# Starting the seven-product projections with one token block, and moving the Fourier values into them

## The chip, the cores and the metric

One core of a Trainium2 chip runs the whole program. The metric is the device time of one execution in microseconds (us), the median of several runs.

## The reference

One encoder layer, on a prompt of 256 tokens and a sample of 2048 tokens with the same weights, width 1024, all in float32. `trunk` is called once for each:

```python
xn = rmsnorm(x, norm_in);  mn = rmsnorm(mem, norm_mem)
pv, pg, fv, fg, q, ag, mg = split_cols(xn @ w_in)      # 1024, 1024, 512, 512, 512, 512, 3072 columns
ya = (pool_mixer(pv, w_pool_grp, pool_scale) * silu(pg)) @ w_pool_out
yb = (fourier_mixer(fv, w_four_grp) * silu(fg)) @ w_four_out
yc = (memory_xattn(q, mn, w_kv) * silu(ag)) @ w_attn_out
ga, gb, gc = split(sigmoid(mg + b_gate), 3)
y = rmsnorm(x + (ga * ya + gb * yb + gc * yc) @ w_o, norm_f)
```

The pooling mixer is a centred window mean less the token, times a matrix per group of 256 columns. The Fourier mixer is the real part of a two-dimensional transform over the tokens and the 128 columns of each of four groups, times a matrix per group. The attention goes to 256 memory tokens per request.

## The kernel before

Every product of two float32 matrices is made of three matmuls on high and low halves (`SPLITS`); making the halves is a cast on ACT and a subtraction on DVE (`split`, lines 98 and 99). The 2304 tokens are nine chunks of 256 and three blocks of 768 (`NB`). The engines' work stands in program order, and each engine works in its order; loads of weights and of intermediate tiles are issued on SP (`st`, line 120), and most stores and loads of intermediate values on POOL's queue.

The stages in order:

- **Opening and Fourier values.** The pooling matrices are multiplied into the pooling columns of `w_in` in 16 steps ("folds", lines 262 to 288, tiles `ptr`, `pvT`, `pfold`, `wfold`), eight at the start and eight at the end of the stage; the result goes to DRAM as `wp_d`. Chunk by chunk the tokens are normalized (`prep`, line 301), turned by eight transposes for each 128 tokens (`transpose8`, line 318) and split into `xc`. The first three chunks' operands go to DRAM as `xq_d`, in the seven combinations that the products later need; the other six chunks go there as plain turned tokens, `xr_d`. The Fourier columns of the chunk are 96 plain matmuls (`fv_mm`, lines 368 to 374), and `fv_post` folds the sample's tokens about their middle into `fe` and `fo`, in SBUF. Four tiles of memory tokens are turned in between.
- **Fourier transform.** Four groups of columns; in each a level of sums (`leaf_odd`, `leaf_even`, on POOL and DVE), short matmuls (`u_step`), the transform's matmuls (`dft_odd`, `dft_even`) and recombination (`comb_odd`, `comb_even`, lines 545 to 591), whose results SP stores to `fo_d`, `fe_d`, `fp_d`.
- **Memory values and keys**: `pv` (line 664) and `pk` (line 680), 96 matmuls each.
- **Products.** The projections go by pairs of weight tiles (class `Pair`, line 779): a 2x2 block product by seven products instead of eight (`PROD`), 12 matmuls of 128x384 each (line 830), accumulated in PSUM tiles x, y and z. There are 26 pairs in each of three blocks, 26 x 7 x 12 x 3 = 6552 matmuls. The x sum of a pair is emptied by ACT (`keep`, line 836) within two products. The activations (`act`, line 843) are Silu and Sigmoid. The Fourier gate multiplies the transform's result there (`gate_four`) and goes to `zb_d`. A small planner puts other work beside the products by its cost (`beside`, `side`, `debt`): the next block's operands (`x_prep`, from `xr_d`) and the pooling mixer (`pooling`) of the block before. `ALONE` and `ORDER` give the order of the seven products within a pair, alone or interleaved with the next pair.
- **Output.** Block by block: the Fourier branch (`pyb`), attention (`ps`), its branch (`pyc`), the pooling branch (`pya`, all line 1095) with gates, the output matrix (`pwo`, line 1290), the residual and the final norm. The mixer of block 2 runs here, in the pooling stage of blocks 0 and 1.

Of the kernel before, what the change touches and what calls it, by code (L numbers as in the profile page):

```python
# [11 lines left out]
F32 = mybir.dt.float32  # L12
# [5 lines left out]
P = 128  # L18
# [3 lines left out]
NB = 3  # L22
# [10 lines left out]
def tile_hybrid_encoder(  # L33
# [23 lines left out]
    def temp(name):  # L57
        return perm.tile([P, D], F32, tag="temp", name=name, bufs=7)
# [23 lines left out]
    vecT = perm.tile([P, 32], F32, tag="vecT", name="vecT")  # L82
# [86 lines left out]
    e_pv, e_fv, e_tok = [[], []], [], {}  # L169
    chunks = [0, 1, 8, 2, 7, 3, 6, 4, 5]  # L170
    MEM_AT = {2: 0, 3: 1, 5: 2, 6: 3}
    e_pv[0].append(st.add(w_in[0:P, PV0:PV0 + 512], 512))
    e_wp = [st.add(w_pool[0:512, :].rearrange("(a p) f -> p a f", p=P))]
    for d in range(1, 8):
        e_pv[0].append(st.add(w_in[d * P:(d + 1) * P, PV0:PV0 + 512], 512))
        if d >= 6:
            e_fv.append(st.add(ftile(w_in, FV0 + (d - 6) * P)))
    e_fv += [st.add(ftile(w_in, FV0 + g * P)) for g in (2, 3)]
    for ci in range(1, len(chunks)):
        for j in range(2):  # L180
# [15 lines left out]
    pairs += [((w_in, Q0 + h * P, "q", h), (w_in, AG0 + h * P, "ag", h)) for h in range(4)]
    for k in (1, 2, 0):
        pairs += [((w_in, MG0 + 1024 * k + c * P, "g", 8 * k + c), (w_in, MG0 + 1024 * k + (c + 4) * P, "g", 8 * k + c + 4))
                  for c in range(4)]
# [9 lines left out]
    n_pair = len(st.src)  # L209

# [32 lines left out]
    fh = rp.tile([P, 4, 4], F32, tag="fh", name="fh")
# [1213 lines left out]
```

## Time and profile before

| | us |
|---|---|
| time, median of three runs | 2136.88 (2136.13 to 2138.97) |
| the profiled execution | 2138.15 |
| its span | 2136.4 |
| TensorE busy | 2066.0 (97%) |
| VectorE (DVE) busy | 1404.8 (66%) |
| ScalarE (ACT) busy | 971.7 (45%) |
| GpSimd (POOL) busy | 421.0 (20%) |

The profile shows one execution; it stands 1.27 us above the median of the runs, and its span leaves out 1.75 us around the program. PE in the trace is TensorE's matmuls, SPq the part of SP that issues DMAs. A row of the timeline gives start, length, engine, line of the kernel, operation, output and inputs, the tile's shape and how often it is repeated; in brackets the idle time before it and what ended it. A group of instructions gives busy us, mean ns of one, and the idle time before them by what ended it. Stages lie at 0 to 191.5 us (opening and values), to 238.6 (transform), to 283.4 (values and keys of the memory), to 1436.7 (products) and to the end.

### The profile page before, as it was taken

What the parts mean: (1) busy time and instruction counts of PE and PEld (TensorE: products, weight loads), DVE (VectorE), ACT (ScalarE), POOL (GpSimd) and SP (SyncE); (2) the same over time, 40 slices, a digit from 0 to 9 for tenths busy, and PEclk for the clock granted to TensorE, in tenths of its full rate; (3) what the DMA queues carried; (4) which work ended last, traced back from release to release, by engine and by line L of the source; (5) the groups of instructions that cost most, each with busy time, mean ns of one, the idle gap of its engine ahead of it and who ended that gap; (6) DMA issues with size and microseconds to landing.
All of it is one profiled execution on the core that took longest, in us unless ns stands there. A gap on an engine that the chain in (4) does not pass through costs nothing. (4 is left out here: it accounts for less than half of the span.)

```text
span 2136.4 us, 31880 instructions
## 1 busy us (share of the span) xinstructions
PE 2066.0 (97%) x12087; PEld 2013.5 (94%) x12087; DVE 1404.8 (66%) x2243; ACT 971.7 (45%) x1785; POOL 421.0 (20%) x700
## 2 busy tenths in 40 slices
PE   7899989999999999999999999998999899999998
PEld 6898879999999999999999999998998899889997
DVE  5765647876555778888656888645675668566553
ACT  5653324655454556555544555546223622344131
POOL 1215213421001244221201212111111111111000
PEclk8999989999999999999999999999999999999999
DMA  8974997975338689676844867457968576876732
GB/s 296 325 231 156 301 235 212 284 207 160 128 121 291 190 243 282 199 220 202 296 143 145 237 199 218 158 200 241 303 209 300 188 261 215 288 237 219 226 118 90
DMA packets 358671, 468.65 MB, mean 219 GB/s; under 512 B 17045, under 2 KB 288437, under 8 KB 358261
## 3 DMA queue, kind: packets, MB, share of 16 engines
q0 software_dynamic: 111952, 261.27, 38.5%
q1 hardware_dynamic: 245792, 203.45, 30.9%
q8 instruction: 95, 1.56, 0.3%
q10 hardware_dynamic: 772, 1.88, 0.3%
q14 instruction: 60, 0.48, 0.1%
HBM read 310.83 MB, written 155.71 MB: 218 GB/s over the span
## 5 line engine op out<-in xcount | busy, mean ns | idle before, releaser
L830 PE MATMUL gx<-xo,wS 128*128 128x384 f32 x2808 | 508.3, 335 | 5.6 <-ACT s L836 4.4
L830 PEld LDWEIGHTS gx<-xo,wS 128*128 128x128 f32 x2808 | 491.0, 189 | 6.5 <-ACT s L836 5.0
L98 ACT CAST hl<-raw 128x1024 fp32r<-128x1024 f32 (+1 forms) x116 | 101.0, 874 | 305.7 <-PE pya L1095 94.3
L1095 PE MATMUL pya<-za,hl 128*128 128x384 f32 x1152 | 200.2, 334 | 0.0
L1095 PEld LDWEIGHTS pya<-za,hl 128*128 128x128 f32 x1152 | 199.7, 188 | 0.0
L830 PE MATMUL gz<-xo,wS 128*128 128x384 f32 x972 | 180.1, 334 | 0.0
L830 PE MATMUL gx<-xo,wA 128*128 128x384 f32 x936 | 170.7, 337 | 7.2 <-DVE kt L99 6.1
L830 PEld LDWEIGHTS gx<-xo,wA 128*128 128x128 f32 x936 | 164.4, 189 | 7.9 <-DVE kt L99 6.5
L830 PEld LDWEIGHTS gz<-xo,wS 128*128 128x128 f32 x972 | 169.7, 188 | 0.0
L99 DVE TENSOR_TENSOR hl<-raw,hl 128x1024 fp32r<-128x1024 f32 (+1 forms) x116 | 115.7, 1000 | 79.4 <-ACT hl L98 79.3
L830 PE MATMUL gy<-xo,wA 128*128 128x384 f32 x900 | 167.1, 334 | 0.0
L830 PE MATMUL gz<-xo,wA 128*128 128x384 f32 x900 | 167.1, 334 | 0.0
L836 ACT COPY u<-gx 128x384 f32<-128x384 f32 x156 | 75.1, 481 | 180.1 <-PE gx L830 179.9
L830 PEld LDWEIGHTS gz<-xo,wA 128*128 128x128 f32 x900 | 157.0, 188 | 0.0
L830 PEld LDWEIGHTS gy<-xo,wA 128*128 128x128 f32 x900 | 157.0, 188 | 0.0
L1290 PE MATMUL pwo<-hl,m 128*128 128x512 f32 x648 | 148.1, 389 | 0.0
L1290 PEld LDWEIGHTS pwo<-hl,m 128*128 128x128 f32 x648 | 121.6, 188 | 25.2
L813 ACT CAST wA<-raw 128x512 fp32r<-128x512 f32 x162 | 98.9, 619 | 70.6 <-PE gy L830 33.3
L817 DVE TENSOR_TENSOR wA<-raw,wA 128x512 fp32r<-128x512 f32 x162 | 109.5, 685 | 31.0 <-ACT wA L813 30.9
L373 PE MATMUL pfv<-xc,fvw 128*128 128x256 f32 x864 | 115.8, 295 | 13.0 <-ACT xc L98 8.2
L817 DVE TENSOR_TENSOR wS<-tb,wS 128x512 fp32r<-128x512 f32 x123 | 83.9, 687 | 64.7 <-ACT wS L813 64.7
L373 PEld LDWEIGHTS pfv<-xc,fvw 128*128 128x128 f32 x864 | 110.8, 201 | 14.8 <-ACT xc L98 9.2
(277 smaller groups left out, 3386.1 us busy)
## 6 DMA issues: line engine op xcount, KB each, us to landing
raw<-in_w_in_dram SPq DMA_DIRECT2D x128, 512.0 KB, 4.3
xo<-xq_d POOLq DMA_DIRECT2D x21, 1536.0 KB, 10.9
g_d<-out POOLq DMA_DIRECT2D x72, 384.0 KB, 2.6
g<-g_d SPq DMA_DIRECT2D x72, 384.0 KB, 4.3
raw<-in_w_o_dram SPq DMA_DIRECT2D x46, 512.0 KB, 4.5
xq_d<-xp POOLq DMA_DIRECT2D x84, 256.0 KB, 3.7
za_d<-za POOLq DMA_DIRECT2D x48, 384.0 KB, 4.7
za<-za_d POOLq DMA_DIRECT2D x24, 768.0 KB, 11.7
```

The source lines that it names most:

```text
L98: nc.scalar.copy(hi, src)
L99: nc.vector.tensor_sub(lo, src, hi.bitcast(F32))
L373: nc.tensor.matmul(o, lhsT=fvw[:, g, a, d * P:(d + 1) * P], rhs=hl[:, :, d // 4, b, (d % 4) * P:(d % 4 + 1) * P], start=(d == 0 and s == 0 ...
L813: nc.scalar.copy(self.ops[op][:, 0, :], self.w[op])
L817: V.tensor_sub(t[:, 1, :], self.w[op], t[:, 0, :].bitcast(F32))
L830: nc.tensor.matmul(o, lhsT=w[:, a, d * P:(d + 1) * P], rhs=x[:, :, c, d, :], start=(first and d == 0 and s == 0), stop=(d == 3 and s == 2) ...
L836: nc.scalar.copy(t, self.ps["x"][:, :384])
L1095: nc.tensor.matmul(ps[:, j, :n], lhsT=w[:, a, d * P:(d + 1) * P], rhs=rhs(c, d, c0, n), start=(d == 0 and s == 0), stop=(d == nd - 1 and s ...
L1290: nc.tensor.matmul(ps[:, hf, :], lhsT=m[d][:, a, lc:lc + P], rhs=w[:, cc, hf * 512:(hf + 1) * 512], start=(d == 0 and (a, cc) == (0, 0)), ...
```

## The change

The opening makes both halves of the folds, and beside them only chunks 0 to 2, whose operands are written to SBUF (`x_norm`, `x_turn`, `x_first`) and not through `xq_d`. The products begin right after it, with a gate's pairs. The Fourier columns are two more pairs ("fv"), 28 in all, so that 28 x 7 x 12 x 3 = 7056 matmuls are products. The tokens of chunks 3 to 8 and the memory tokens are loaded, scaled, turned (`turn4`, four transposes into one PSUM buffer "gt") and split beside the products of the block before (`Task`, `x_chunk`, `mem_tile`); PSUM buffers of y go from two to one, half tiles from four to three, temporaries from seven to six. The mixer of four tiles of block 2 runs beside block 2's last products, the other four in the pooling stage of block 0. The Fourier gate and values are stored as they are (`fg_d`, `fv_d`). Memory values and keys and then the transform come after the products; `fold_in` loads the values of a group and folds them, and `make_zb` loads gate and transform for the output stage, gates and splits them.

The diff, cut to what matters (the functions of the transform moved without a change but for `fe`, `fo`, `fp` being tiles per group; the key and value matmuls moved as they were):

```diff
...
+    pg = [two("pg", w_in, PG0 + c * P, c, None, PG0 + (c + 4) * P, c + 4) for c in range(4)]
+    qa = [two("q", w_in, Q0 + h * P, h, "ag", AG0 + h * P, h) for h in range(4)]
+    fg = [two("fg", w_in, FG0 + g * P, g, None, FG0 + (g + 2) * P, g + 2) for g in range(2)]
+    fv = [two("fv", w_in, FV0 + g * P, g, None, FV0 + (g + 2) * P, g + 2) for g in range(2)]
+    pv = [two("pv", wp_d, c * P, c, None, (c + 4) * P, c + 4) for c in range(4)]
+    gt = [two("g", w_in, MG0 + 1024 * k + c * P, 8 * k + c, None, MG0 + 1024 * k + (c + 4) * P, 8 * k + c + 4)
+          for k in (1, 2, 0) for c in range(4)]
+    pairs = gt[:4] + pg + fg + qa + fv + pv + gt[4:]
 
     NP = len(pairs)
-    rest = list(range(NP))
-    orders = [rest, rest[-2:] + rest[:-2], rest[-4:-2] + rest[:-4] + rest[-2:]]
+    every = list(range(NP))
+    iv = every[16:20]
+    rest = [i for i in every[:-2] if i not in iv]
+    orders = [every, every[-2:] + iv + rest, rest[-2:] + iv + rest[:-2] + every[-2:]]
...
-    def fv_mm(hl, ps, groups):
-        for g in groups:
-            o = flat(ps)[:, g * 256:(g + 1) * 256]
-            for d in range(8):
-                for s, (a, b) in enumerate(SPLITS):
-                    nc.tensor.matmul(o, lhsT=fvw[:, g, a, d * P:(d + 1) * P], rhs=hl[:, :, d // 4, b, (d % 4) * P:(d % 4 + 1) * P],
-                                     start=(d == 0 and s == 0), stop=(d == 7 and s == 2))
...
+    def x_first(c):
+        r = [x_turn(2 * c + j).rearrange("p (h f) -> p h f", h=2) for j in range(2)]
+        x11, x21, x12, x22 = r[0][:, 0], r[0][:, 1], r[1][:, 0], r[1][:, 1]
+        ta, tb = (ls.tile([P, 2, 512], F32, tag="rt", name=f"xt{c}_{k}", bufs=4) for k in range(2))
+        for o, v, a, b in ((0, x11, None, None), (4, ta[:, 1], x22, x12), (3, ta[:, 0], x12, x11),
+                           (5, tb[:, 0], x22, ta[:, 0]), (2, x21, None, None), (1, x22, None, None),
+                           (6, tb[:, 1], x21, tb[:, 0])):
+            if a is not None:
+                V.tensor_sub(v, a, b)
+            q = xop[o][:, c].rearrange("p a d t -> p a (d t)")
+            split(q[:, 0], q[:, 1], v)
+
+    fold_w(0)
...
+    x_norm(0)
+    x_norm(1)
+    for n in range(16):
+        nxt = fold_tr((n + 1) // 8, (n + 1) % 8) if n < 15 else None
+        fold_mm(n // 8, n % 8, hl)
         hl = nxt
...
+        if n == 0:
+            for i in range(2, 6):
+                nc.sync.dma_start(x0[i], x_rows(i))
+            x_first(0)
+        elif n == 1:
+            x_norm(2)
+            x_norm(3)
+        elif n == 2:
+            x_first(1)
+        elif n == 3:
+            x_norm(4)
+            x_norm(5)
+        elif n == 4:
+            x_first(2)
+        elif n == 7:
+            fold_w(1)
```

```diff
...
+    def token_scale(ts, nm):
+
+        n = len(ts)
+        ss, ms, sd, y, t2, r = (col(f"{nm}_{q}", n) for q in ("ss", "ms", "sd", "y", "t", "r"))
+        junk = temp(f"j{nm}")
+        for j in range(n):
+            nc.scalar.activation(junk, ts[j], AF.Square, accum_out=ss[:, j:j + 1])
+            yield 0, 1
+        V.tensor_scalar(out=ms, in0=ss, scalar1=1.0 / D, scalar2=EPS, op0=ALU.mult, op1=ALU.add)
+        yield 0.1, 1
+        nc.scalar.activation(sd, ms, AF.Sqrt)
+        yield 0, 1
+        V.reciprocal(y, sd)
+        V.tensor_mul(t2, y, y)
+        V.scalar_tensor_tensor(out=t2, in0=t2, scalar=-0.5, in1=ms, op0=ALU.mult, op1=ALU.mult)
+        V.scalar_tensor_tensor(out=r, in0=t2, scalar=1.5, in1=y, op0=ALU.add, op1=ALU.mult)
+        yield 0.3, 1
+        for j in range(n):
+            nc.scalar.activation(ts[j], ts[j], AF.Copy, scale=r[:, j:j + 1])
+            yield 0, 1
+
+    def turn4(t, ds, nm):
+        ps = psg.tile([P, 512], F32, tag="gt", name=f"pt{nm}", bufs=1)
+        for i, d in enumerate(ds):
+            nc.tensor.transpose(ps[:, i * P:(i + 1) * P], t[:, d * P:(d + 1) * P], ident)
+        return ps
...
+    def x_chunk(c, ts, ahead):
+
+        yield from token_scale(ts, f"x{c}")
         for e in range(2):
             x = temp(f"xl{c}_{e}").rearrange("p (o f) -> p o f", o=4)
 
-            src = xr_d[c - 3].rearrange("p (j h e f) -> p j h e f", j=2, h=2, e=2)
-            nc.gpsimd.dma_start(x[:, 0:2, :], src[:, :, 0, e, :])
-            nc.gpsimd.dma_start(x[:, 2:4, :], src[:, ::-1, 1, e, :])
-            yield 0, 5
+            for j in range(2):
+                ds = (2 * e, 2 * e + 1, 4 + 2 * e, 5 + 2 * e)
+                ps = turn4(ts[j], ds, f"{c}_{e}_{j}")
+                yield 0, 1
+                if e and j:
+                    ahead()
+                for i, d in enumerate(ds):
+                    o = ((0, 3), (1, 2))[j][i // 2]
+                    nc.scalar.activation(x[:, o, (i % 2) * P:(i % 2 + 1) * P], ps[:, i * P:(i + 1) * P], AF.Copy,
+                                         scale=vecT[:, 32 + d:33 + d])
+                yield 0, 1
             t = temp(f"xt{c}_{e}").rearrange("p (o f) -> p o f", o=4)
...
-    ALONE = (1, 7, 6, 2, 5, 3, 4)
+    ALONE = ((1,), (7,), (6,), (2, 5), (3,), (4,))
...
+        if b + 1 < NB and i == 0:
+            todo += [Task(lambda c=c: x_load([2 * c, 2 * c + 1], "x"), lambda t, ahead, c=c: x_chunk(c, t, ahead))
+                     for c in range(3 * (b + 1), 3 * (b + 2))]
+        if b == 0 and i == 0:
+            todo += [Task(lambda m=m: x_load([m], "m"), lambda t, ahead, m=m: mem_tile(m, t, ahead)) for m in range(4)]
+        if b > 0 and i == 7:
+            todo += [pool_task(b - 1, c) for c in POOL_C]
+            if b == NB - 1:
+                todo += [pool_task(b, c) for c in POOL_C[:4]]
+        return todo
```

```diff
...
+    mn_t = [rm.tile([P, 2, 2, 512], F32R, tag=f"mn{i}", name=f"mn{i}") for i in range(4)]
...
+    for i in range(4):
+        for a in range(2):
+            nc.gpsimd.dma_start(mn_t[i][:, a], ms_d[a, 256 * i:256 * (i + 1), :].rearrange("(d p) t -> p d t", p=P))
+    nc.gpsimd.dma_start(cs, t_cs)
+    def fold_in(g):
+
+        v = lm.tile([P, T], F32, tag="v", name=f"fv{g}")
+        nc.sync.dma_start(v, fv_d[g])
+        e = lm.tile([P, 1026], F32, tag="fe", name=f"fe{g}", bufs=2)
+        o = lm.tile([P, 1024], F32, tag="fo", name=f"fo{g}", bufs=2)
+        s = v[:, SP_:]
+        V.tensor_add(e[:, 1:1024], s[:, 1:1024], s[:, 2047:1024:-1])
+        V.tensor_sub(o[:, 1:1024], s[:, 1:1024], s[:, 2047:1024:-1])
+        nc.scalar.copy(e[:, 0:1025:1024], s[:, 0:1025:1024])
+        p = lm.tile([P, SP_], F32, tag="fp", name=f"fp{g}", bufs=2)
+        nc.scalar.copy(p, v[:, :SP_])
+        fe[g], fo[g], fp[g] = e, o, p
+
+    fold_in(0)
...
+    make_csw()
+    ho = leaf_odd(0)
+    he, hm = leaf_even(0)
+    fold_in(1)
...
+    for g in range(4):
+        po = dft_odd(g, uo)
+        if g < 2:
+            fold_in(g + 2)
+        if g < 3:
+            uo = u_step(g + 1, ho, CS8, "o")
+        comb_odd(g, po)
+        if g < 2:
+            ho = leaf_odd(g + 2)
+        pe = dft_even(g, ue, um)
+        if g < 3:
+            ue, um = u_step(g + 1, he, CSE, "e"), u_step(g + 1, hm, (0, 0, 1), "m")
+        comb_even(g, *pe)
+        if g < 2:
+            he, hm = leaf_even(g + 2)
...
-    def load_zb(b, eng=nc.gpsimd):
-        return [load_z(0, f"zb{b}_{g}", zb_d[g], b, eng) for g in range(4)]
+    def make_zb(b, g):
+        f, sg = ld_tile(lw, f"four{b}_{g}", 5), load_cols(fg_d[g], f"fgl{b}_{g}", b)
+        load_four(f, g, b)
+        gate_four(sg, f, b)
+        z = zt(0, f"zb{b}_{g}")
+        z_split(z, sg[:, :TB])
+        return z
...
-        zb = load_zb(0, nc.sync)
-        at.load_q(0, nc.sync)
-        st.load_upto(eb[0]["yb"][3])
-        at.load_q(1, nc.sync)
+    at.load_q(0)
+    at.load_q(1)
     at.load(0)
     at.load(1)
+    st.load_upto(eb[0]["yb"][3])
+    zb = [make_zb(0, g) for g in range(4)]
...
+            if c % 2 and b == 0:
+                pc = POOL_C[4 + c // 2]
...
+                if not last and gr == 0 and d % 2:
+                    zb.append(make_zb(b + 1, d // 2))
```

How it moves the order of the instructions, at three places.

TensorE where the products begin; `gx`, `gz` are the PSUM sums of a pair, `xo` an operand of the tokens, `wA` and `wS` of the weights, `pk` the keys. Before:

```order
L680 MATMUL pk_2967<-mn_2021,hl_2903 128x512 x6
L680 MATMUL pk_2967<-mn_2022,hl_2903 128x512 x6
L680 MATMUL pk_2967<-mn_2023,hl_2903 128x512 x6
L680 MATMUL pk_2967<-mn_2717,hl_2903 128x512 x6
L830 MATMUL gx_0_3043<-xo_0_2720,wA_0_0_3019 128x384 x12
L830 MATMUL gx_1_3059<-xo_0_2720,wA_0_0_3019 128x384 x12
L830 MATMUL gz_0_3078<-xo_4_2722,wS_0_0_3027 128x384 x12
L830 MATMUL gz_1_3098<-xo_4_2722,wS_0_0_3027 128x384 x12
```

and now:

```order
L282 MATMUL pfold_5_712<-wpl_t,pvT_5_685 128x256 x12
L270 MATMUL ptr_7_728<-ident,raw_638 128x128 x4
L282 MATMUL pfold_6_736<-wpl_t,pvT_6_709 128x256 x12
L282 MATMUL pfold_7_752<-wpl_t,pvT_7_733 128x256 x2
L340 MATMUL pvec<-ident,vrow 128x48
L282 MATMUL pfold_7_752<-wpl_t,pvT_7_733 128x256 x10
L483 MATMUL gx_0_817<-xo_0_100,wA_0_0_793 128x384 x12
L483 MATMUL gx_1_833<-xo_0_100,wA_0_0_793 128x384 x12
L483 MATMUL gz_0_852<-xo_4_101,wS_0_0_801 128x384 x12
L483 MATMUL gz_1_872<-xo_4_101,wS_0_0_801 128x384 x12
```

The first products stand behind the last step of the folds instead of the keys, and the vectors' transpose between them.

POOL's queue where the products end; `out` is a pair's result, `k` the keys, `mn` the normalized memory tokens. Before:

```order
L849 DMA g_d<-out_2_24_13838 128x768
L849 DMA g_d<-out_2_25_13857 128x768
L849 DMA g_d<-out_2_24_13839 128x768
L849 DMA g_d<-out_2_25_13858 128x768
L1121 DMA k_0_0_14114<-kv_d 128x512
L1121 DMA k_0_1_14116<-kv_d 128x512
L1121 DMA k_1_0_14118<-kv_d 128x512
L1121 DMA k_1_1_14120<-kv_d 128x512
```

and now:

```order
L502 DMA g_d<-out_2_26_12786 128x768
L502 DMA g_d<-out_2_27_12805 128x768
L502 DMA g_d<-out_2_26_12787 128x768
L502 DMA g_d<-out_2_27_12806 128x768
L816 DMA mn_13052<-ms_d 128x2x512 x2
L816 DMA mn_13053<-ms_d 128x2x512 x2
L816 DMA mn_13054<-ms_d 128x2x512 x2
L816 DMA mn_13055<-ms_d 128x2x512 x2
L817 DMA cs<-in_t_cs_dram 128x512
```

Where the loads of the keys for the output stood behind the last gate stores, the loads of the memory tokens do.

SP's queue where the transform ends; `fo_d`, `fe_d`, `fp_d` are its results in DRAM, `fgl` the stored gate, `four` the tile that takes the result of a group, `zb` the gated values. Before, the end of the transform and, 150 rows on, the start of the output:

```order
L556 DMA fo_d<-fo_2669 128x1024
L585 DMA fe_d<-fe_2693 128x1024
L591 DMA fp_d<-pcp_2703 128x256
L120 DMA raw_2776<-in_w_kv_dram 128x8x128
L120 DMA raw_3011<-wp_d 128x8x128
```

```order
L120 DMA raw_13709<-in_w_in_dram 128x8x128
L1070 DMA zb_0_14093<-zb_d 128x2x768
L1070 DMA zb_1_14095<-zb_d 128x2x768
L1070 DMA zb_2_14097<-zb_d 128x2x768
L1070 DMA zb_3_14099<-zb_d 128x2x768
L1070 DMA q_0_14101<-q_d 128x2x768
```

and now:

```order
L919 DMA fo_d<-fo_13828 128x1024
L948 DMA fe_d<-fe_13852 128x1024
L954 DMA fp_d<-pcp_13862 128x256
L1060 DMA fgl_0_13905<-fg_d 128x768
L398 DMA four_0_13904<-fp_d 128x256
L399 DMA four_0_13904<-fe_d 128x256
L400 DMA four_0_13904<-fo_d 128x256
L1060 DMA fgl_1_13917<-fg_d 128x768
L398 DMA four_1_13916<-fp_d 128x256
L399 DMA four_1_13916<-fe_d 128x256
L400 DMA four_1_13916<-fo_d 128x256
```

The loads for the gated values follow the last group's three stores directly, in one queue, where weights and a finished `zb_d` were loaded; on TensorE the first matmuls behind the transform are those of `pyb`, which need `zb` of group 0.

## Rows read from the trace of the kernel before

**Rows 1.** Windows: us; busy PE, PEld, DVE, ACT, POOL; clock; DMA share; GB/s.

```profile
0.00:191.53 191.53, 169.07 (x1320) 165.14 (x1321) 114.94 (x210) 102.75 (x163) 43.24 (x79) 0.95 0.82 264
191.53:238.59 47.06, 39.00 (x330) 37.62 (x329) 40.96 (x57) 17.36 (x30) 28.12 (x51) 1.00 0.62 198
238.59:283.42 44.83, 43.82 (x196) 35.97 (x194) 16.84 (x24) 10.95 (x15) 7.92 (x11) 1.00 0.99 302
283.42:1436.65 1153.23, 1141.53 (x6552) 1140.09 (x6552) 817.74 (x1386) 592.56 (x1109) 264.43 (x430) 0.99 0.69 207
1436.65:2136.40 699.75, 672.59 (x3697) 634.64 (x3696) 414.30 (x568) 248.05 (x469) 77.29 (x131) 0.99 0.67 224
```

**Rows 2.** Lines by form, PE: values, folds; busy us, mean ns, idle before.

```profile
L373 PE MATMUL pfv<-xc,fvw 128*128 128x256 f32 x864 | 115.8, 295 | 13.0 <-ACT xc L98 8.2 <-DVE xc L99 3.8 <-DVE rx_ms L224 0.9
L284 PE MATMUL pfold<-wpl_t,pvT 128*128 128x256 f32 x192 | 29.7, 306 | 0.2 <-DVE pvT L99 0.2
```

**Rows 3.** Windows of line 830 alone, a stretch without a wait.

```profile
327.15:720.00 392.85, 392.85 (x2268) 392.85 (x2268) 1.00 0.66 199
```

**Rows 4.** Timeline of PE: start, length; transposes between the values' matmuls.

```profile
63.93 1.04 PE L318 MATMUL pxt<-ident,xnx 128*128 128x128 f32 x8
64.72 2.15 PE L373 MATMUL pfv<-xc,fvw 128*128 128x256 f32 x16
```

**Rows 5.** Timeline of PE in the opening.

```profile
3.74 1.09 PE L272 MATMUL ptr<-ident,raw 128*128 128x128 f32 x4 [3.74 <-DMA raw<-in_w_in_dram]
37.34 11.02 PE L373 MATMUL pfv<-xc,fvw 128*128 128x256 f32 x68 [1.18 <-DVE xc L99]
```

**Rows 6.** Timeline of PE where the products begin.

```profile
283.42 2.34 PE L830 MATMUL gx<-xo,wA 128*128 128x384 f32 x12 [1.01 <-PE pk L680]
291.91 4.16 PE L830 MATMUL gx<-xo,wA 128*128 128x384 f32 x12 [6.15 <-DVE kt L99]
```

**Rows 7.** Lines by form, ACT then DVE: pieces of the opening.

```profile
L98 ACT CAST pvT<-ptr 128x512 fp32r<-128x512 f32 x16 | 9.4, 589 | 16.0 <-PE ptr L272 16.0
L301 ACT ACTIVATE xnx<-raw 128x1024 f32<-128x1024 f32 x16 | 17.1, 1067 | 0.9 <-ACT xc L98 0.9
L287 ACT COPY wfold<-pfold 128x512 f32<-128x512 f32 x16 | 9.4, 586 | 9.1 <-PE pfold L284 9.0
L99 DVE TENSOR_TENSOR pvT<-ptr,pvT 128x512 fp32r<-128x512 f32 x16 | 11.0, 688 | 14.3 <-ACT pvT L98 14.1
L303 DVE SCALAR_TENSOR_TENSOR xnx<-raw,rx_r,nin 128x1024 f32<-128x1024 f32 x16 | 20.6, 1285 | 0.6
```

**Rows 8.** Timelines of ACT, POOL and PE where the products end.

```profile
1437.48 0.93 ACT L843 ACTIVATE out<-out,vecT 128x768 f32<-128x768 f32 x1 [1.15 <-DVE out L899]
1438.71 0.54 POOL L849 DMA_DIRECT2D g_d<-out  x1 [1.54 <-ACT out L843]
1438.98 6.04 PE L1095 MATMUL pyb<-zb,hl 128*128 128x384 f32 x24 [2.17 <-ACT hl L98]
1447.42 0.98 PE L1142 MATMUL ps<-k,q 128*128 128x256 f32 x6 [2.39 <-DMA k<-kv_d]
```

**Rows 9.** Tile mn, last row: from issue to landing of its loads.

```profile
DMA to landing us min/median/max: 3.9/4.7/8.4
```

**Rows 10.** Page, part 6: KB of one load, us from issue to landing.

```profile
g<-g_d SPq DMA_DIRECT2D x72, 384.0 KB, 4.3
```

**Rows 11.** Timelines of PE and SP's queue where the Fourier stage ends.

```profile
238.59 22.05 PE L664 MATMUL pv<-hl,mn 128*128 128x512 f32 x96
243.56 0.36 SPq L591 DMA_DIRECT2D fp_d<-pcp  x1
```

**Rows 12.** Timeline of DVE inside the Fourier stage.

```profile
200.74 3.84 DVE L501 TENSOR_TENSOR heven<-E 128x256 f32<-128x256 f32 x1
```

**Rows 13.** Lines of ACT and waits of PE, 315 to 1430 us.

```profile
L843 ACT ACT_TABLE_LOAD x6 | 7.7, 1283 | 0.1
PE gx L830 <- ACT s L836: 1.2, 1, 1.2
```

More of the change, by code (lines that the diff above doesn't have):

```diff
@@ L196, in tile_hybrid_encoder @@
[L196 to L199, printed above, removed]
+    e_pv, e_wp = [[], []], []
+    for h in range(2):
+        e_wp.append(st.add(w_pool[512 * h:512 * (h + 1), :].rearrange("(a p) f -> p a f", p=P)))
+        for d in range(8):
+            e_pv[h].append(st.add(w_in[d * P:(d + 1) * P, PV0 + 512 * h:PV0 + 512 * (h + 1)], 512))
@@ new lines, in tile_hybrid_encoder, with __init__, load, x_load @@
+    class Task:
+        def __init__(self, load, gen):
+            self.fetch, self.gen, self.got = load, gen, None
+        def load(self):
+            if self.got is None:
+                self.got, self.at = self.fetch(), now[0]
+    def x_load(rows, kind):
+        ts = []
+        for i in rows:
+            t = la.tile([P, D], F32, tag="xt", name=f"{kind}t{i}", bufs=2)
+            nc.gpsimd.dma_start(t, x_rows(i) if kind == "x" else m_rows(i))
+            ts.append(t)
+        return ts
@@ new lines, in tile_hybrid_encoder @@
+    side, debt, run = [], 0.0, None
+    OWN = {"A11": 0.3, "S3": 0.6, "S2": 0.95, "S4": 0.6, "A22": 0.3, "A12": 0.3, "S1": 0.3}
+    AHEAD = 7
+    hand = {getattr(mybir.EngineType, e) for e in ("PE", "DVE", "Activation")}
+    with tc.manual_schedule(engines=hand):
+        for k in range(-AHEAD, len(seq) + 4):
+            now[0] = k
+            if 0 <= k < len(seq):
+                q, p = seq[k]
+                q.mm(p)
+            if 0 < k <= len(seq):
+                q, p = seq[k - 1]
+                q.post(p)
+                if p in (5, 2, 4):
+                    debt += 0.27
+            for f in later.pop(k, ()):
+                f()
+            for n, stage in ((7, "sums"), (6, "high"), (5, "low")):
+                if 0 <= k + n < len(seq):
+                    q, p = seq[k + n]
+                    getattr(q, stage)(PROD[p][1])
+                    if stage == "sums":
+                        debt += OWN[PROD[p][1]]
+            if not 0 <= k < len(seq):
+                continue
+            q, p = seq[k]
+            if p == 1:
+                side += beside(q.b, q.k)
+            debt = max(0.0, debt - 1.0)
+            while debt < 0.8:
+                if run is None:
+                    if not side:
+                        break
+                    task = side.pop(0)
+                    task.load()
+                    run = task.gen(task.got, side[0].load if side else (lambda: None))
+                    ready = task.at + 6
+                if ready > k:
+                    break
+                step = next(run, None)
+                if step is None:
+                    run = None
+                else:
+                    debt += step[0]
+                    ready = k + step[1]
+            o = PROD[p][2]
+            if q.b + 1 < NB and last_use[q.b, o] == k:
+                load_xop(q.b + 1, o)
+        assert not later
```

964 lines of the change are left out of this document (380 added, 584 removed).

## Prediction

> **What bounds the kernel now.** First the busy time by stage. Five windows cut the span where TensorE passes from one stage to the next: opening with the Fourier values, Fourier transform, memory keys and values, products, output [rows 1]. TensorE is busy 169.1 + 39.0 + 43.8 + 1141.5 + 672.6 = 2066.0 of 2136.4 us, so the kernel is bound by TensorE, and 70 us stand idle: 22.5 in the opening, 8.1 in the transform, 11.7 in the product window, 27.1 in the output. Then what a product costs where nothing waits: 2268 matmuls in 392.85 us, 0.1732 us each, and a product of 12 takes 2.08 us [rows 3]. So a change pays if it takes matmuls away, or idle time at the seams; it costs where it makes new seams. The reader should look at the seams last: each is a chain over other engines and a trip through DRAM.
>
> **The change, part by part**, against the span 2136.4.
>
> 1. *Opening.* The values' 864 matmuls, 115.8 us busy with 13.0 us idle before them, and the turning of chunks 1 to 8 leave it [rows 2]; both fold halves and chunks 0 to 2 stay. What bounds it then is ScalarE or VectorE, not TensorE, which has 16 fold steps of 29.7/16 = 1.86 us [rows 2]. ScalarE, by rows 7: 16 casts and 16 copies of the fold (9.4 + 9.4), six squares (6.4) and six copies of about the same size (6.4), 21 casts of operand pieces at 0.589 (12.4), 2 at twice that (2.4): 46.4. VectorE: 11.0 for the folds, six scalings (7.7), 21 low halves and 12 sums at 0.688 (22.7), two of twice that (2.8), and small ones: some 46. The first matmul starts at 3.74 [rows 5], so the products cannot begin before 3.7 + 46.4 = 50. Upper end: before, chunk 0 and the first fold half together had the first values running at 37.34 [rows 5]; two more chunks of 2 x 1.285 + 4 x 0.688 + 7 x 0.688 = 10.1 us of VectorE each, and then eight fold steps of 1.86, give 37.3 + 20.3 + 14.9 = 73. I take 62: the second fold half stands last in TensorE's order, behind a chain that starts at about 10 and has three chunks of some 12 us, 10 + 36 + 15 = 61, and one for the first weight's halves. So 62 instead of 191.5: **-129.5** (-141 to -118).
>
> 2. *Products.* Two Fourier-value pairs more: 28 x 7 x 12 x 3 = 7056 matmuls, 7056 x 0.1732 = 1222.1. 128 transposes now stand between products. Between the values' matmuls eight took 64.72 - 63.93 = 0.79 us [rows 4], so 128 cost 12.7. Starting up: the first product took 2.34 for 2.08 and one after an idle time 4.16 [rows 6]; I take 3. Waits: the long stretch has 1.2 us now [rows 13]. One PSUM buffer fewer for y, three half tiles instead of four and ten more jobs on ScalarE speak for more; I take 4 (2 to 15). VectorE is 71% and ScalarE 51% busy in the window [rows 1], which covers their added work as an average. Together 1241.8 instead of 1153.2: **+88.6** (+86 to +100).
>
> 3. *Products to keys.* Before, keys ended and products began on loads long made; now the norms of the memory are loaded on POOL's queue behind the last four gate stores. At the old end of the products the last matmul ended at 1438.98 - 2.17 = 1436.81, ScalarE's last gate at 1438.41, and POOL issued at 1438.71 for 0.54 [rows 8]. Two stores and the first load's issue end about 1440.3, and a load lands after 4.7 (3.9 to 8.4) [rows 9]: idle some 8.2. Then TensorE comes from an idle time as in rows 6, where 12 matmuls lost 2.1: 2.5. **+10.7** (+9 to +15).
>
> 4. *Keys.* The same 43.8 busy of 44.8, without the idle 1.0, with six short matmuls for the transform's small matrix: **+0.5**.
>
> 5. *Transform.* Its window is 47.1 with VectorE 41.0 busy [rows 1]. Folding the sample about its middle, which the values' epilogue did chunk by chunk, comes in: two VectorE operations of 1023 elements per group, two groups inside the window. At 0.688 for 512 [rows 7] that is 4 x 1.3 = 5.2, and 0.8 for POOL's leaves, now behind the key stores. Zero if it hides beside TensorE's 39.0; twice as much if it is stretched, as one 256-element operation was to 3.84 here [rows 12]. **+6** (0 to +12).
>
> 6. *Transform to output.* TensorE's next work in order is the Fourier branch's projection, and it needs the gated values of group 0. Their four loads stand on SP behind the stores of the last group. Before, TensorE left the transform at 238.59 and the last of these stores was issued by 243.56 + 0.36 = 243.92 [rows 11], 5.3 later, hidden behind the keys. Now nothing covers it. Then four issues of 0.36 (1.4), landing (4.3 for a larger load [rows 10]), the last gated piece and a high half (0.93 for 768 columns [rows 8]), about 0.4 + 0.9: idle 12.3, where 2.17 is today [rows 8]. Add 1.5 until groups 1 to 3 follow and 2.5 as in 3; the wait for k of 2.39 [rows 8] falls away, since k is loaded long before. 10.1 + 1.5 + 2.5 - 2.4: **+11.7** (+6 to +18).
>
> 7. *Output*: the matmuls are the same. The next block's gated values are made beside the last projection, the mixer of four tiles moves from there into the products. VectorE is busy 414 of 700 us, ScalarE 248 [rows 1]: **0**. Without that cover it would cost a few us per block, part of the rivals below.
>
> Sum: -129.5 + 88.6 + 10.7 + 0.5 + 6 + 11.7 = -12.0, span 2124.4. The profiled execution took 2138.15, 1.75 above its span and 1.27 above the median of 2136.88: 2126.15 for such an execution, **2125** for the median. A measurement of this kernel can tell about 0.2%, 4.3 us: faster is below 2132.6, slower above 2141.2.
>
> **Rivals.**
>
> *The seams cost more.* Three stages that lay apart by work of TensorE now hang on one another through DRAM. If the loads of the memory land at 8.4 instead of 4.7 and those of group 0 as late [rows 9], that is 3.7 + 4.1, and 1 or 2 more for the groups behind: 2134 (2133 to 2141), no difference that can be told. For it: all these loads start together when a stage begins. Against: rows 9 and 10 are medians of loads under traffic. An opening of 73 ends in the same place, 2125 + 11 = 2136.
>
> *The opening is cheaper.* If ScalarE and VectorE run without gaps, 50 to 54: 2113 to 2117, and if the folding also hides in the transform, 2107 to 2111. Against it: the gaps of ScalarE in the fold now, 16.0 and 9.1 us [rows 7].
>
> *ScalarE falls behind in the products, and the kernel is slower.* It empties the x sums of every pair, and TensorE needs that buffer two products later: 4.16 us. Into its order come six chunks and four memory tiles; each has a square root, whose table is loaded and then the gate's again: 2 x 1.283 = 2.57 us [rows 13], beside squares of 1.07 and small scaled copies. That is under 4.16, so alone it reaches TensorE nowhere, and the wait for ScalarE in the products today is 1.2 us in all [rows 13]. It decides once ScalarE is already 1.6 us late when such a load comes. If all ten reach TensorE whole, 10 x 2.57 = 26: 2125 + 26 = 2151, slower. For it: three half tiles, so that a late store holds ScalarE back. Against: 51% busy [rows 1].
>
> By the Trainium skill ("ScalarE: Activation LUTs", What ACT_TABLE_LOAD costs), a switch to another table costs a load of about 1283 ns and a drain of about 1380 ns, 2.66 us together. The rows agree on the load and don't show the drain. By that rule the pair would be 5.3 us, 1.2 us over the 4.16 in each of ten jobs, an estimate of 12 us, which would give 2137. It would add to the weight of this rival; with six loads and almost no wait today the trace has not borne it out.
>
> **How the numbers follow.** The forecast, 2114 to 2133: 0.58. The cheap opening, below 2114: 0.08. Costly seams or the slow opening, 2133 to 2141: 0.17. ScalarE late, 2142 to 2160: 0.17. So faster 0.66, same 0.17, slower 0.17. Range: the summed bounds of the terms, taken as independent, are about -14 and +18; 2110 to 2142 leaves out the most favourable corner (0.04) and nearly all of the last rival (0.16).
>
> **What would show it.** First product of line 483 near 62 us. From there 1242 us to the last one, with 0.173 us per matmul in a stretch, and waits of TensorE on ScalarE under 4 us in total; ten groups of waits next to table loads would show the third rival. Between products and keys one gap of about 8, released by the loads of the memory; after the transform one of about 12, released by group 0's gated values; VectorE busy for over 45 us in the transform. Wrong would be: a gap over 15 at either seam, a product window over 1255, or a first product after 75.

## The result, and the profile after

The changed kernel took 2168.89 us (median of four runs, 2166.17 to 2169.70), the kernel before 2137.93: 1.0143 times as long, with an interval of 1.0126 to 1.0161. It is slower by 31 us where 12 us less were forecast. The profiled execution took 2168.86 with a span of 2167.0.

The windows of the changed kernel, cut at the same borders as [rows 1] (opening; products; memory values and keys; transform; output). The columns are as there.

```profile
0.00:70.21 70.21, 44.27 (x305) 41.10 (x306) 45.26 (x90) 45.10 (x81) 8.96 (x21) 0.88 0.59 198
70.21:1328.40 1258.19, 1256.09 (x7186) 1253.77 (x7184) 883.72 (x1509) 713.88 (x1373) 248.45 (x418) 1.00 0.63 195
1328.40:1388.35 59.95, 46.98 (x198) 38.69 (x199) 23.66 (x23) 13.28 (x19) 26.33 (x42) 0.89 0.93 290
1388.35:1440.34 51.99, 43.20 (x345) 41.48 (x343) 43.42 (x62) 18.33 (x33) 28.83 (x47) 0.97 0.41 134
1440.34:2167.00 726.66, 686.20 (x3697) 642.72 (x3696) 417.47 (x584) 251.32 (x471) 61.58 (x103) 0.98 0.64 212
```

The opening ends at 70.2 us instead of 191.5. The products last 1258.2, the keys with the gap ahead of them 60.0, the transform 52.0, and the output with the gap ahead of it 726.7. The five windows have TensorE busy for 2076.7 us in all, 10.7 more than before, although 115.8 us of plain matmuls are gone and only 504 x 0.1732 = 87.3 us of products have come in their place. By these two numbers alone it should have been busy for 28 us less.

The larger part of the reason stands in the row that answers to [rows 3]: line 483 alone, in a stretch without a wait.

```profile
700.00:1100.00 400.00, 400.00 (x2280) 400.00 (x2279) 1.00 0.60 194
```

2280 matmuls in 400.00 us are 0.1754 us each, where [rows 3] had 392.85/2268 = 0.1732, at the same granted clock of 1.00. TensorE is busy in the whole stretch, so it is not a wait that comes and goes: the matmuls themselves take longer, on the mean.

The waits of TensorE over the whole span (us in total, times, longest), and those inside the products:

```profile
PE pyb L1071 <- ACT zb L98: 18.7, 1, 18.7
PE pv L975 <- DMA mn<-ms_d: 13.0, 1, 13.0
PE pxt L298 <- DVE rx_ms L217: 10.8, 2, 5.5
PE ptr L270 <- DMA raw<-in_w_in_dram: 10.2, 2, 9.5
```

```profile
PE gx L483 <- DVE wA L470: 2.1, 2, 1.7
```

Two seams cost 18.7 and 13.0 us, the opening has 21 us of waits, and 1258 us of products have 2.1. ScalarE's table loads in the same stretch number 22, where [rows 13] had six:

```profile
L496 ACT ACT_TABLE_LOAD x14 | 18.0, 1283 | 0.3
L575 ACT ACT_TABLE_LOAD x8 | 10.3, 1283 | 0.1
```

No wait of TensorE stands beside them, so the rival that had the kernel slower for ScalarE's sake is not what happened.

### The profile page after: what moved, and what is told of

Same layout as the page of the kernel before. It is cut to its first block, busy times and chain, and to the rows that moved or that the text cites. A ratio compares the mean times of both kernels' runs of the same rounds, so it can differ in the third digit from the quotient of the medians.

```text
span 2167.0 us, 31239 instructions
## 1 busy us (share of the span) xinstructions
PE 2076.7 (96%) x11727; PEld 2017.7 (93%) x11727; DVE 1413.5 (65%) x2266; ACT 1041.9 (48%) x1977; POOL 374.1 (17%) x629
## 4 chain that ended last, share of the span: by engine, by line
PE 80%; issue 11%; DVE 4%; POOL 2%; DMA 2%; ACT 1%; SPq 0%; POOLq 0%; DVEq 0%; ACTq 0%
PE gx L483 26%; PE gz L483 13%; PE pya L1071 9%; PE pwo L1265 9%; PE gy L483 6%; PE pyc L1071 5%; PE pyb L1071 4%; PE po L1158 1%; PE pv L975 1%; PE pk L995 1%; PE ps L1118 1%; DMA raw<-in_w_in_dram 1%; PE pfold L282 1%; POOL za_d L392 1%; DMA four<-fp_d 0%
## 5 line engine op out<-in xcount | busy, mean ns | idle before, releaser
L483 PE MATMUL gx<-xo,wS 128*128 128x384 f32 x2880 | 528.3, 338 | 0.0
L483 PEld LDWEIGHTS gx<-xo,wS 128*128 128x128 f32 x2880 | 506.7, 188 | 0.0
L483 PE MATMUL gx<-xo,wA 128*128 128x384 f32 x1152 | 213.8, 340 | 2.1 <-DVE wA L470 2.1
L483 PEld LDWEIGHTS gx<-xo,wA 128*128 128x128 f32 x1152 | 203.7, 189 | 3.0 <-DVE wA L470 2.7
L1071 PE MATMUL pya<-za,hl 128*128 128x384 f32 x1152 | 203.2, 338 | 0.0
L483 PE MATMUL gz<-xo,wS 128*128 128x384 f32 x1044 | 196.6, 339 | 0.0
L483 PE MATMUL gy<-xo,wA 128*128 128x384 f32 x972 | 184.3, 338 | 0.0
L483 PE MATMUL gz<-xo,wA 128*128 128x384 f32 x972 | 183.3, 338 | 0.0
L1265 PE MATMUL pwo<-hl,m 128*128 128x512 f32 x648 | 152.3, 395 | 0.0
L1265 PEld LDWEIGHTS pwo<-hl,m 128*128 128x128 f32 x648 | 121.6, 188 | 29.3
L1071 PE MATMUL pyb<-zb,hl 128*128 128x384 f32 x576 | 111.6, 351 | 25.2 <-ACT zb L98 18.7
L545 DVE TENSOR_TENSOR out<-u,gz 128x384 f32<-128x384 f32 x84 | 46.5, 553 | 135.7 <-PE gz L483 135.3
L1071 PEld LDWEIGHTS pyb<-zb,hl 128*128 128x128 f32 x576 | 106.3, 197 | 27.0 <-ACT zb L98 18.9
## 6 DMA issues: line engine op xcount, KB each, us to landing
za<-za_d POOLq DMA_DIRECT2D x24, 768.0 KB, 11.7
```

The costliest lines, as they stand in the source:

```text
L483: nc.tensor.matmul(o, lhsT=w[:, a, d * P:(d + 1) * P], rhs=x[:, :, c, d, :], start=(first and d == 0 and s == 0), stop=(d == 3 and s == 2) ...
L545: V.tensor_add(o1[:, :, 0, :], v(self.u2), v(self.ps["z"]))
L1071: nc.tensor.matmul(ps[:, j, :n], lhsT=w[:, a, d * P:(d + 1) * P], rhs=rhs(c, d, c0, n), start=(d == 0 and s == 0), stop=(d == nd - 1 and s ...
L1265: nc.tensor.matmul(ps[:, hf, :], lhsT=m[d][:, a, lc:lc + P], rhs=w[:, cc, hf * 512:(hf + 1) * 512], start=(d == 0 and (a, cc) == (0, 0)), ...
```

## The experiments

**Where the tiles lie.** One line of the change had not been looked at: a small tile on the left side of SBUF, which holds vectors, got twice its width.

```diff
-    vecT = perm.tile([P, 32], F32, tag="vecT", name="vecT")
+    vecT = perm.tile([P, 64], F32, tag="vecT", name="vecT")
```

The tiles allocated after it on the left that matmuls read start 128 bytes later in each partition (the temporary that fell away moves some of them back by 4096, a multiple of 256). Those on the right, counted from the other end, stay. In the two built programs the tiles that the matmuls read start here (byte in the partition, and its remainder modulo 256):

```
                                   before           after
weights wA, wS, hl (left)          33920   128      34048     0
tokens xo of the products (right)  143232  128      143232  128
za, zb, zc, m of the output (right) 149376 128      149376  128
memory tokens mn                   87680   128      167424    0
```

Before, both operands of every large matmul began at the same remainder. Now weights and tokens lie 128 bytes apart, except for the memory's, where both lie at 0. In the trace of the changed kernel the memory's matmuls (`pk`) did not become slower. Lines by form (busy us, mean ns of one), first two of the kernel before, then those of the changed kernel:

```profile
L1095 PE MATMUL pya<-za,hl 128*128 128x384 f32 x1152 | 200.2, 334 | 0.0
L1290 PE MATMUL pwo<-hl,m 128*128 128x512 f32 x648 | 148.1, 389 | 0.0
```

```profile
L1071 PE MATMUL pya<-za,hl 128*128 128x384 f32 x1152 | 203.2, 338 | 0.0
L1265 PE MATMUL pwo<-hl,m 128*128 128x512 f32 x648 | 152.3, 395 | 0.0
L995 PE MATMUL pk<-mn,hl 128*128 128x512 f32 x96 | 21.9, 389 | 0.0
L1118 PE MATMUL ps<-k,q 128*128 128x256 f32 x216 | 30.2, 294 | 1.3 <-DMA q<-q_d 0.9 <-DVE partial L1213 0.4
```

Two matmuls of the same 128x512: 389 ns for `pk`, 395 for `pwo`, which had 389 before as well. That made the theory, and there is an unused tile on the right by which it can be tried alone.

*The changed kernel, right side moved by 128 bytes.*

```diff
-    pad.tile([P, 24], F32, tag="pad", name="pad")
+    pad.tile([P, 56], F32, tag="pad", name="pad")
```

> The changed kernel with the unused tile on the right side of SBUF made 56 wide instead of 24, so that every tile of the right side lies 128 bytes lower. In the kernel before, the tiles of both sides that matmuls read began at the same remainder modulo 256 bytes (128); the change widened a small tile on the left by 128 bytes, so that weights lie at 0 and the moving tokens at 128. Theory A (this distance makes each matmul slower): a matmul of 128x384 in a stretch goes back from 0.1756 to 0.1732 us, 1141 matmuls in 200 us become 1155, the products' window shortens by 17 us, the output's by 11, the whole by 26 to 30: 2141. Theory B (ScalarE and the DMA traffic beside the products slow the matmuls): spacing stays 0.1756, 2169. Theory C (this chip is slower than the one of the first runs): the kernel before is slower too when it is run beside it, and this one stays at 2169.

Measured: 2139.64 (ten runs), 1.0004 times the kernel before beside it (0.9993 to 1.0015). The stretch and the forms:

```profile
700.00:1100.00 400.00, 400.00 (x2309) 400.00 (x2308) 1.00 0.60 192
```

```profile
L1071 PE MATMUL pya<-za,hl 128*128 128x384 f32 x1152 | 200.2, 334 | 0.0
L1265 PE MATMUL pwo<-hl,m 128*128 128x512 f32 x648 | 148.1, 389 | 0.0
L995 PE MATMUL pk<-mn,hl 128*128 128x512 f32 x96 | 22.6, 395 | 0.0
L1118 PE MATMUL ps<-k,q 128*128 128x256 f32 x216 | 30.3, 295 | 3.0 <-DMA q<-q_d 2.5 <-DVE partial L1213 0.5
```

2309 matmuls where there were 2280: 0.1732 us again. `pya` is back from 203.2 to 200.2 and `pwo` from 152.3 to 148.1. The edit also moved `mn`, on the right, to 128 while `hl` stays at 0, and there `pk` rises from 389 to 395: a control that was not planned. The scores `ps` (128x256, keys on the left, queries on the right) are alike at both distances, 30.2 and 30.3. Theory A holds: 29 us are gone with one number.

*The kernel before with the same edit.*

> The kernel before with the same edit: the right side 128 bytes lower, so that weights lie at 128 and tokens at 0. Theory A: 6552 + 2304 matmuls of 128x384 get 2.4 ns each and 864 of 128x512 get 6.6 ns, 21 + 6 = 27 us, and the 864 of the values something between 1 and 4 us: 2163 to 2169. Theories B and C: no change, 2138.

Measured: 2162.38 (2157.76 to 2165.68), 1.0103 times (1.0077 to 1.0128), by a change of one unused tile's width. The stretch is that of [rows 3]:

```profile
327.15:720.00 392.85, 392.85 (x2234) 392.85 (x2233) 1.00 0.66 197
```

```profile
L1095 PE MATMUL pya<-za,hl 128*128 128x384 f32 x1152 | 203.2, 338 | 0.0
L1290 PE MATMUL pwo<-hl,m 128*128 128x512 f32 x648 | 152.3, 395 | 0.0
L373 PE MATMUL pfv<-xc,fvw 128*128 128x256 f32 x864 | 116.9, 296 | 12.8 <-ACT xc L98 8.2 <-DVE xc L99 3.8 <-DVE rx_ms L224 0.7
L284 PE MATMUL pfold<-wpl_t,pvT 128*128 128x256 f32 x192 | 28.9, 302 | 0.4 <-DVE pvT L99 0.2 <-ACT pvT L98 0.2
```

2234 matmuls instead of 2268, 0.1758 each; `pya` 203.2, `pwo` 152.3, as in the changed kernel. The time stands just under the 2163 to 2169 expected, which counted 1 to 4 us for the 864 matmuls of the values. But their operands, `fvw` and `xc`, both lie on the left and did not move apart: 116.9 for the 115.8 of [rows 2] is no effect of distance. The operands of the folds did move apart, to 128, and `pfold` took 28.9 for 29.7. So the cost needs neither the changed order nor the traffic beside the products, nor is it the chip: the kernel before, unedited, took 2139.22 (median) beside it.

*The left side moved instead.*

> The changed kernel with the small tile that the change widened made wider still (96 columns), so that the left side moves by another 128 bytes and weights lie at 128 again, as tokens do. If only the distance of weights and tokens counts: matmuls of 128x384 at 0.1733 us, 2138 to 2141. If the address of one of them counts (tokens must lie at 0): 0.1757, 2169.

```diff
-    vecT = perm.tile([P, 64], F32, tag="vecT", name="vecT")
+    vecT = perm.tile([P, 96], F32, tag="vecT", name="vecT")
```

Measured: 2139.35, 1.0004 times the kernel before (0.9993 to 1.0015), 2309 matmuls in the stretch. Weights and tokens both at 128, as before, or both at 0: no difference. It is the distance that counts.

*Distances of 64, 32 and 96* (the unused tile 40, 48 and 32 wide).

> The changed kernel with the unused tile 40 wide, so that the right side moves by 64 bytes: tokens at 64, weights at 0. Theory A in its strict form (any distance costs): slow, 2160 to 2170. Theory A in its coarse form (only a distance of 128 costs, or only the number of 256-byte rows that a read touches): between 2141 and 2169, told by the spacing. Theories B and C: 2169.

> The changed kernel with tokens at 32 and weights at 0 modulo 256. At a distance of 64 the matmuls of 128x384 ran at 0.1734 and those of 128x512 at 0.2328, at 128 at 0.1757 and 0.2322. If the cost grows with the distance: 0.1734 and 0.227 to 0.230, 2139 to 2142. If every distance other than 0 costs the wide ones the same: 0.2328, 2142 to 2145.

> The changed kernel with tokens at 96 and weights at 0. If the cost of the 128x384 sets in between 64 and 128 in steps: 0.1734 or 0.1757, nothing between, 2142 or 2168. If it grows smoothly: 0.1742 to 0.1750, 2152 to 2162.

The first was timed in ten runs; of the other two there is one time each. For each kernel the table has the matmuls of line 483 in the 400 us, and the busy us of the 1152 `pya` (128x384) and the 648 `pwo` (128x512).

| weights, tokens | products | pya | pwo | time |
|---|---|---|---|---|
| 0, 0 | 2309 | 200.2 | 148.1 | 2139.64 |
| 0, 32 | 2310 | 204.0 | 152.3 | 2151.52 |
| 0, 64 | 2310 | 200.2 | 152.3 | 2144.04 |
| 0, 96 | 2266 | 204.0 | 152.9 | 2178.65 |
| 0, 128 | 2280 | 203.2 | 152.3 | 2168.89 |

In `pwo` the tokens `m` are the operand that TensorE holds (`lhsT`) and the weights the one that streams; in the products and `pya` it is the other way round.

Both guesses on 32 and on 96 missed: the cost neither grows with the distance nor sets in at one step. At 32 the products run free and `pya` does not, although both are 128x384; in the code the products read the tokens in three pieces of 128 columns and `pya` in one of 384. Of the distances tried only 0 was free for all three. What the reads of weights and tokens do to each other inside SBUF stays open.

**The two seams.** The places of TensorE's first matmuls behind each, and what the queues and engines did there in the changed kernel:

```profile
1341.37 23.98 PE L975 MATMUL pv<-hl,mn 128*128 128x512 f32 x96 [12.97 <-DMA mn<-ms_d]
1459.07 1.01 PE L1071 MATMUL pyb<-zb,hl 128*128 128x384 f32 x2 [18.73 <-ACT zb L98]
```

```profile
1331.19 3.58 POOL L816 DMA_DIRECT2D mn<-ms_d  x5
```

```profile
1444.53 0.66 SPq L954 DMA_DIRECT2D fp_d<-pcp  x1
1445.37 0.50 SPq L1060 DMA_DIRECT2D fgl<-fg_d  x1
1447.08 0.49 SPq L400 DMA_DIRECT2D four<-fo_d  x1
```

```profile
1457.06 1.10 DVE L413 TENSOR_TENSOR fgl<-fgl,four 128x256 f32<-128x256 f32 x3 [12.59 <-DMA four<-fp_d]
```

```profile
1334.00:1338.00 4.00, 0.00 (x0) 0.00 (x0) 0.00 (x0) 0.00 (x0) 2.89 (x5) 0.50 1.06 398
1450.00:1454.00 4.00, 0.00 (x0) 0.00 (x0) 0.00 (x0) 0.00 (x0) 0.00 (x0) 0.50 1.11 387
```

```profile
DMA to landing us min/median/max: 10.1/12.1/16.5
```

The issues stand where the forecast had them: the memory's loads start 2.8 us behind the last product (1324.03 + 4.37; by the forecast the first issue was to end 3.5 behind it, and it takes 3.58/5 = 0.7), and the last store of the transform is issued by 1445.19, 4.9 us behind TensorE's last matmul of the transform (1439.96 + 0.38; 5.3 was forecast). What is late is the landing. The quickest of the memory's loads took 10.1 us, and the gating of group 0 began 9.5 us after the last of its four loads was issued. In these stretches the DMA share is 1.06 and 1.11, at 398 and 387 GB/s: weights, Fourier values, keys, queries and a norm vector go out at the same moment as what TensorE waits for.

*The order in the queues changed*, at 128 bytes of distance (`make_zb` and its loads take the queue as an argument):

```diff
-        nc.sync.dma_start(v, fv_d[g])
+        (nc.gpsimd if g == 0 else nc.sync).dma_start(v, fv_d[g])
...
     at = Attention(0)
+    zb = [make_zb(0, g, nc.gpsimd) for g in range(2)]
     at.load_q(0)
-    at.load_q(1)
     at.load(0)
+    zb += [make_zb(0, g, nc.gpsimd) for g in (2, 3)]
+    at.load_q(1)
     at.load(1)
     st.load_upto(eb[0]["yb"][3])
-    zb = [make_zb(0, g) for g in range(4)]
```

> The changed kernel; the load of the Fourier values for group 0 goes on POOL's queue behind the memory's loads instead of beside them on SP, and the loads for the gated values of block 0 go on POOL's queue ahead of the keys and queries instead of behind the last group's stores on SP. Theory D (the two gaps of 13.0 and 18.7 us come from the order of transfers in the queues, the needed ones sharing the DMA engines with those needed later): 13.0 becomes 7 to 9 and 18.7 becomes 6 to 9, 2169 becomes 2152 to 2156. Theory E (the DMA engines are full at these seams whatever the order): each gap moves by less than 3 us, 2164 to 2169. The spacing of the matmuls stays 0.1756.

Measured: 2158.84 (2158.55 to 2159.64), 10 less than without the edit and between the ranges of both theories. The 400 us of line 483 hold 2281 matmuls, as without the edit. Its waits, and the DMA share at the first seam:

```profile
PE pv L975 <- DMA mn<-ms_d: 10.2, 1, 10.2
PE pyb L1071 <- ACT zb L98: 8.8, 4, 6.1
PE pyb L1071 <- ACT pe L1127: 5.4, 3, 2.2
```

```profile
1334.00:1338.00 4.00, 0.00 (x0) 0.00 (x0) 0.00 (x0) 0.00 (x0) 3.58 (x6) 0.50 1.05 312
```

The gap behind the transform fell from 18.7 to 6.1, as theory D has it: loads that need not stand behind the last group's stores are best issued before them. The one behind the products fell only from 13.0 to 10.2, as theory E has it for this seam: the share is still 1.05 there with the Fourier values out of the way. The gates' last stores and two weight tiles go out just ahead of the memory's loads, and what they cost was not tried apart. Of the 15 us some 5 were given back behind: group by group TensorE waits for gated values (8.8 in four pieces, the gap of 6.1 among them) and for the softmax (5.4, was 3.2).

**The opening.** In the changed kernel the first weights land late, and the products begin behind the last fold step. From TensorE's timeline:

```profile
9.48 1.08 PE L270 MATMUL ptr<-ident,raw 128*128 128x128 f32 x4 [9.48 <-DMA raw<-in_w_in_dram]
12.07 2.66 PE L282 MATMUL pfold<-wpl_t,pvT 128*128 128x256 f32 x12
44.41 1.94 PE L298 MATMUL pxt<-ident,x 128*128 128x128 f32 x8 [0.46 <-DVE x L293]
70.21 0.51 PE L483 MATMUL gx<-xo,wA 128*128 128x384 f32 x2
```

*Another order, with both sides at the same remainder:*

```diff
-    nc.sync.dma_start(x0[0], x_rows(0))
     st.load_upto(1)
+    nc.sync.dma_start(x0[0], x_rows(0))
...
-        elif n == 1:
             x_norm(2)
             x_norm(3)
-        elif n == 2:
+        elif n == 4:
             x_first(1)
-        elif n == 3:
             x_norm(4)
             x_norm(5)
-        elif n == 4:
+        elif n == 9:
             x_first(2)
-        elif n == 7:
+        if n == 7:
             fold_w(1)
```

Beside this the first weight tile stands ahead of the pooling matrix in the list of loads.

> The changed kernel with both sides of SBUF at the same remainder (as in the run before last with 2139.6) and another opening: the first weight tile is loaded ahead of the first tokens and the pooling matrix, and chunks 1 and 2 are normalized and turned after fold steps 0, 4 and 9 instead of 0 to 4, so that VectorE's work on the tokens lies beside TensorE's second fold half. Theory F (the opening of 70 us is late because fold steps of TensorE stand in a row behind the tokens' chain, and because the first weights land at 9.5): first product at 59 to 64 us, 2129 to 2135. Theory G (VectorE and ScalarE set its length in any order): first product at 68 to 71, 2138 to 2140.

Measured: 2133.04 (2131.86 to 2135.48), 0.9973 times the kernel before (0.9962 to 0.9985). The same places, but for the turning of tokens:

```profile
6.37 1.09 PE L271 MATMUL ptr<-ident,raw 128*128 128x128 f32 x4 [6.37 <-DMA raw<-in_w_in_dram]
12.22 2.91 PE L283 MATMUL pfold<-wpl_t,pvT 128*128 128x256 f32 x12
64.54 2.63 PE L482 MATMUL gx<-xo,wA 128*128 128x384 f32 x14
```

The first product stands at 64.5 instead of 70.6 (the kernel with the places mended), half a microsecond outside the range of theory F, and far from G. The first weights land 3.1 us earlier, but the first fold matmul stands at 12.2 as it did at 12.1: it is the order of the fold steps and the tokens' work that cost 6 us.

**All three together**, and nothing else.

> The same with the two edits at the seams as well (the load of the Fourier values behind the memory's, the gated values' loads on POOL's queue ahead of keys and queries), which by themselves took 10 us away at 128 bytes of distance. If the three savings are independent: 2139.6 - 10 - 5 to 10, 2119 to 2125, faster than the kernel before by 0.7 to 0.9%. If the later stages give back what the opening gains (for instance because the first products then wait for their weights): 2127 to 2132.

Measured: 2123.35 (2121.32 to 2126.48) against 2139.13 for the kernel before beside it, 0.9927 times (0.9914 to 0.9939). This version beats both. From the changed kernel's 2168.89 the places of the tiles take 29.3, the opening 6.6, the order in the queues 9.7.

## Why the prediction was wrong, point by point

The windows of the changed kernel with both sides at the same remainder, cut as above, tell the terms of the sum apart from the tiles' places. TensorE is busy for 2048.5 us in them, 17.5 less than before; the keys (48.1 for 43.8) and the transform (44.2 for 39.0) take more of it.

```profile
0.00:70.61 70.61, 44.41 (x306) 41.48 (x306) 44.83 (x89) 45.17 (x81) 8.96 (x21) 0.88 0.58 194
70.61:1315.13 1244.52, 1241.25 (x7186) 1238.81 (x7184) 883.67 (x1509) 713.60 (x1373) 248.40 (x418) 1.00 0.64 197
1315.13:1376.30 61.17, 48.12 (x198) 38.84 (x199) 23.70 (x23) 13.27 (x19) 26.34 (x42) 0.89 0.94 285
1376.30:1428.29 51.99, 44.23 (x345) 42.66 (x343) 43.42 (x62) 18.33 (x33) 28.83 (x47) 0.93 0.40 133
1428.29:2139.50 711.21, 670.46 (x3696) 632.13 (x3696) 417.44 (x584) 251.25 (x471) 61.56 (x103) 0.98 0.65 217
```

| term of the sum | forecast | changed kernel | places mended |
|---|---|---|---|
| 1, opening | -129.5 | -121.3 | -120.9 |
| 2, products | +88.6 | +105.0 | +91.3 |
| 3 and 4, first seam and keys | +11.2 | +15.1 | +16.3 |
| 5, transform | +6 | +4.9 | +4.9 |
| 6 and 7, second seam and output | +11.7 | +26.9 | +11.5 |
| sum | -12.0 | +30.6 | +3.1 |

- **The step that failed: "a product of 12 takes 2.08 us" carried into the changed kernel**, and with it "the matmuls are the same" for the output. The duration was read right from [rows 3] but taken as belonging to the shape. It belongs to the shape and to the places of both operands. The change widened a tile by 128 bytes, of which no term spoke, and 7056 + 2304 matmuls of 128x384 and 864 of 128x512 became 1.3 to 2.8% longer. 13.7 us of it lie in the products (1258.2 against 1244.5) and 15.5 in the output (726.7 against 711.2), where 17 and 11 were expected of the mended run. This took the kernel out of the range and made it slower, and none of the rivals had it. It is not the whole miss: with the places mended the kernel is level with the one before (1.0004, and 3.1 us between the two profiled spans), not 12 us faster, and the other 15 us lie in the terms below, the opening above all. Of the prediction's own signs of being wrong two came: a product window over 1255 and a gap over 15.
- **Opening, 8 us short.** 62 was forecast and 70.2 came, within the bounds of 50 to 73. The tokens' chain ended where the forecast had it: the last turning at 44.41 + 1.94 = 46.3, forecast 10 + 36. But eleven fold steps stood behind it and not eight, since chunk 2 is turned behind the fifth of the 16, and they took 23.9 us and not 15. With six steps behind it, the experiment had the first product at 64.5. That the first weights landed at 9.5, where [rows 5] had 3.74, is not what it hung on.
- **Products, but for the places, right** to 3 us. The transposes, the extra pairs, one PSUM buffer for y and three half tiles made TensorE wait for 2.1 us, below the 4 taken.
- **ScalarE late: did not happen.** 22 table loads of 1283 ns, and TensorE's waits in the products, 2.1 us, are for VectorE. The Trainium skill ("ScalarE: Activation LUTs", What ACT_TABLE_LOAD costs) gives about 1283 ns for a load and about 1380 ns for a drain with it; the trace agrees on the load and does not show the drain. The estimate of 1.2 us of TensorE per job that the prediction worked out from both did not come.
- **First seam, 5 us short.** The chain up to the issue was right, the landing was 10.1 and not 4.7: [rows 9] has loads under the traffic of a stage that runs, and at a seam everything is issued at once. The rival of costly seams had this cause. Without the places 2139.6 would have lain in its range, though not by this cause alone: of the 15 us the first seam brought 5 and the opening 8.6.
- **Second seam, right only in the sum, and by luck.** The idle time was 18.7 and not 12.3, for the same reason. The rest of the output was 5 us shorter than before (711.2 - 18.8 = 692.4 against 697.4); the waits for k are gone from it, and where the remainder comes from was not tried.
- **Transform right to 1 us**: VectorE is busy for 43.4 of its 52.0 us, where over 45 were forecast.

## What to carry to other kernels

Before a matmul's duration is carried into a changed kernel, compare where weights and moving operand start in SBUF: any change of a tile's width moves all that is allocated behind it, and here 128 bytes cost 29 us, as much as the 28 us of matmuls that the change takes away. A longer mean matmul without waits, at the same granted clock, was the mark of it, and 128 bytes more of an unused tile mended it. At a new seam price the landing of the needed load by all that is issued in the same microseconds, not by its median under load, and issue first what the next stage reads first.

## What the runs showed of the hardware that was not expected

A matmul's duration depends on the distance, modulo 256 bytes, between the starts of its two operands in a partition: for the products' 128x384 at 0 (both at 0 or both at 128) 0.1732 us, and the same at 32 and 64; at 128 0.1754 to 0.1758; at 96 0.1765 (400/2266). For 128x512 every other distance that was tried cost 2.8 to 3.2% (152.3 to 152.9 us for 648, where 0 took 148.1). For 128x256 no cost shows at 128 (`ps` 30.2 against 30.3, `pfold` 28.9 against 29.7). DVE's operations kept their durations (the 174 low halves `wA<-raw,wA` of line 470 took 685 ns each at both distances). The Trainium skill ("SBUF — State Buffer", Who interferes with whom) gives TensorE two read ports, one for the moving operand and one for loading weights, independent of each other. No run here shows ports; but here a matmul's duration is not independent of how its two operands lie to each other, and there the measurement decides.
